# Three attentions: products with the values over pairs of query blocks

## Chip, core and metric

One core of one Trainium2 chip runs the whole program. The metric is device time in microseconds from the first to the last instruction, as the median of the runs.

## What is computed

Two transformer blocks, batch 1, 1024 tokens, width 1024, all in 32-bit floats. Three attentions stand in them, each worked in query blocks of 128 rows. The change touches only their last step, the product of the attention weights with the values:

```python
# first block, 16 heads of 64: stick-breaking attention, per query block i
a = where(mask, exp(log_beta + suffix), 0.0)        # mask: kpos < qpos
out = einsum('bhqk,bhkd->bhqd', a, vb)              # keys 0 .. end of block i
# second block: sliding window, 8 heads of 64, 2 groups of keys and values
probs = softmax(concat([scores, sink]))[..., :-1]   # keys of blocks n-1 and n
out = einsum('bnkgqs,bnskd->bnqkgd', probs, vb)
# second block: differential attention, 4 heads, values 128 wide
a = p[:, :, 0] - lam * p[:, :, 1]                   # two softmaxes, keys 0 .. end of block n
out = einsum('bhqs,bshe->bqhe', a, v)
```

Everything around them (projections, gates, a short convolution, a feed-forward part, norms) is the same before and after.

## The kernel before, in words

**Order of the work.** The program is written twice by `tile_body`: a dry pass learns how long each buffer lives, the second one writes the instructions. Both run a clock of their own (`Sched`, line 57 on): `note` (L153) adds an assumed cost to the engine of each instruction, and side tasks (generators) are woken when that clock says their inputs are there (`when`, L86; `turn` of `Sched`, L107). The main line of the program is the projections (`proj`, tile `pj`): between two of their matmuls, side tasks that are due slip in their own. So the costs in `note` fix the order of instructions on every engine, and on the chip each engine runs its list in that order, waiting where it must. Where the main line needs a side task to be done it stands still (`sch.until`): line 2272 for the first half of stick-breaking attention, 2281 for its second half, 2286 and 2292 for the two halves of the second block's attentions. While it stands, TensorE gets side work alone.

**The attentions.** `attention_1` runs `stick` (L1068) for tokens 0 to 511 and then 512 to 1023; `attention_2` runs `swa` (L1233) and `diff` (L1314) for the first half and then for the second. `crew` (L1035) keeps at most two to four units of work alive. A unit of `stick` is one of 8 pairs of heads `p`, a query block `i` and a head `h`. It makes scores on TensorE (tile `z`), two sigmoids on ScalarE (`om`, `be`; up to 512 keys both stand in one tile `ob`), a running product and a product on VectorE, turns the 128x128 blocks of `be` with TensorE (`turn`, L1009, tile `tr`), copies them to `aT` on ScalarE, and when both heads of a block are there multiplies:

```python
for kb in range(n):
    r = slice(0, 127 if kb == n - 1 else 128)
    for hh in range(2):
        mm(po[64 * hh:64 * hh + 64, (i % 4) * 128:(i % 4 + 1) * 128],
           lhsT=vt[r, kb * 128 + 64 * hh:kb * 128 + 64 * hh + 64],
           rhs=got[hh][r, kb * 128:(kb + 1) * 128], start=kb == 0, stop=kb == n - 1)
```

The values (`vt`, tile `vp`) are the stationary operand, 64 columns of the array for each head; `po` (tile `o`) holds four query blocks. `swa` does the same with two key blocks per query block and values from `vas`. `diff` uses all 128 columns: a unit is a head and a query block, with two softmaxes (scores and a row maximum in one VectorE instruction, shown as CUSTOM; `Exp` on ScalarE; scale-and-add on VectorE), then `turn` and the products. After a head's four blocks, `sub_norm` (L1399) sums squares with TensorE (tile `sm`), takes a root, spreads it (tile `rb`) and hands the head to the next projection. A plain 32-bit product is two TensorE instructions.

**Room.** Wide tiles come from 34 buffers; `room` (L312) holds a unit or a load back until enough are free.

Of the kernel before, what the change touches and what calls it, by code (L numbers as in the profile page):

```python
# [57 lines left out]
class Sched:  # L58
# [94 lines left out]
    def note(self, eng, op, out, args, extra=0.0):  # L153
# [111 lines left out]
def tile_body(  # L265
# [46 lines left out]
    def room(n, hold=0):  # L312

        while in_use[0] + n > N4:
            yield 0.4
        in_use[0] += hold
# [692 lines left out]
    def turn(src, n):  # L1009
# [10 lines left out]
        yield dst  # L1020
        return dst

    def fetched(loads, keys, need, fetch, tiles, ahead=1):
# [44 lines left out]
    def stick(live, half, width, rho):  # L1068
# [4 lines left out]
        def work(p, i, h):  # L1073
# [13 lines left out]
            for c0, c1 in CUTS[n]:  # L1087
# [17 lines left out]
            aT = yield from turn(be, n)  # L1105
            free()
            got = st.setdefault((p, i), {})
            got[h] = aT
            if len(got) < 2:
                return  # L1110
            if p not in st:
                yield from sch.a_bank()
# [10 lines left out]
            free(2 * (w > HT))  # L1123
            del st[p, i]
            st[p][1] += 1
            if st[p][1] == 3 and ("z", p, half) in flags:
# [106 lines left out]
    def swa(live, half, width, rho):  # L1233
# [15 lines left out]
        def work(t, n):  # L1249
# [35 lines left out]
            pT = yield from turn(p, 4)  # L1285
# [6 lines left out]
            blocks = [(0, n - 1), (1, n)] if n else [(0, 0)]  # L1292
            for a, (b, kb) in enumerate(blocks):
                for h in range(2):
                    mm(po[64 * h:64 * h + 64, (n % 4) * 128:(n % 4 + 1) * 128],
                       lhsT=vas[0][:, kb, 64 * g:64 * g + 64],
                       rhs=pT[:, (2 * h + b) * 128:(2 * h + b + 1) * 128],
                       start=a == 0, stop=a == len(blocks) - 1)
            st[t][1] += 1
            if st[t][1] == 4:  # L1300
                del loads[t], st[t]
                loads["done"].add(t)
# [11 lines left out]
    def diff(live, half, width, rho):  # L1314
# [43 lines left out]
        def work(h, i):  # L1358
            yield from arrived(loads, h)
            n = i + 1  # L1360
            w = n * 128
            yield from room(3 * (w > HT), 3 * (w > HT))
            p0, l0 = yield from softmax(h, i, 0)
            vec.tensor_scalar(out=p0[:, 0:w], in0=p0[:, 0:w], scalar1=l0[:, 0:1], scalar2=None, op0=ALU.mult)
            p1, l1 = yield from softmax(h, i, 1)
# [7 lines left out]
                loads["done"].add(h)  # L1373
                free(3 + half)
            yield p0
            aT = yield from turn(p0, n)
            free(w > HT)
            if h not in st:
                yield from sch.a_bank()
            if h not in st:  # L1380
# [7 lines left out]
            free(w > HT)  # L1388
            st[h][1] += 1
            if st[h][1] == 4:  # L1390
                del st[h], vts[h]
                free(half)
# [941 lines left out]
```

## Time and profile before

| what | value |
|---|---|
| median of 3 runs | 2580.68 us (2580.65 to 2581.55) |
| the profiled execution | 2582.41 us, its span 2580.6 us |
| granted TensorE clock, mean | 0.991 of full speed |
| TensorE matmuls busy | 97% of the span |
| VectorE, ScalarE, GpSimd busy | 69%, 49%, 19% |
| HBM traffic over the span | 253 GB/s |

A busy share is that of time in which at least one instruction of the engine was in flight. TensorE's matmuls overlap one another by their latency, so for the cost of one the distance between two starts counts, and not its length.

### The profile page before, as it was taken

What the parts mean: (1) busy time and instruction counts of PE and PEld (TensorE: products, weight loads), DVE (VectorE), ACT (ScalarE), POOL (GpSimd) and SP (SyncE); (2) the same over time, 40 slices, a digit from 0 to 9 for tenths busy, and PEclk for the clock granted to TensorE, in tenths of its full rate; (3) what the DMA queues carried; (4) which work ended last, traced back from release to release, by engine and by line L of the source; (5) the groups of instructions that cost most, each with busy time, mean ns of one, the idle gap of its engine ahead of it and who ended that gap; (6) DMA issues with size and microseconds to landing.
All of it is one profiled execution on the core that took longest, in us unless ns stands there. A gap on an engine that the chain in (4) does not pass through costs nothing.

```text
span 2580.6 us, 38805 instructions
## 1 busy us (share of the span) xinstructions
PE 2505.5 (97%) x13215; PEld 2057.5 (80%) x13215; DVE 1792.8 (69%) x3245; ACT 1255.7 (49%) x2529; POOL 490.0 (19%) x894
## 2 busy tenths in 40 slices
PE   7999999989999899998999999999999899999998
PEld 6888888879877677787888887888888678788887
DVE  7866666777697788986765556774666876677555
ACT  5311112555455677677664353564634634345442
POOL 0012112312101002331211321222222222221000
PEclk9999999999999999999999999999999999999999
DMA  9867869857897665775876978977886987978764
GB/s 283 264 190 201 203 214 280 235 185 249 279 274 222 204 163 157 221 192 140 250 217 160 262 209 261 260 226 220 200 237 217 237 225 235 238 225 252 226 201 130
DMA packets 541726, 570.43 MB, mean 221 GB/s; under 512 B 32910, under 2 KB 410008, under 8 KB 541528
## 3 DMA queue, kind: packets, MB, share of 16 engines
q1 hardware_dynamic: 482644, 381.99, 50.3%
q0 software_dynamic: 56528, 181.75, 25.3%
q10 hardware_dynamic: 2356, 4.21, 0.4%
q8 instruction: 104, 1.70, 0.3%
q14 instruction: 94, 0.77, 0.1%
HBM read 466.90 MB, written 186.91 MB: 253 GB/s over the span
## 4 chain that ended last, share of the span: by engine, by line
PE 65%; DVE 5%; DMA 3%; ACT 2%; issue 2%; SPq 0%; POOL 0%; DVEq 0%; ACTq 0%; POOLq 0%
PE pj L249 53%; PE o L249 4%; PE z L249 4%; PE tr L250 3%; DVE om L250 2%; PE pv L249 1%; DMA wr<-sg_d2g 1%; DVE be L250 1%; DVE wl L250 1%; DMA wr<-in_b_w_out_dram 1%; DVE ob L250 1%; DVE act L250 0%; DVE fa L250 0%; ACT om L250 0%; ACT be L250 0%
## 5 line engine op out<-in xcount | busy, mean ns | idle before, releaser
L249 PE MATMUL pj<-act,wh 128*128 128x512 f32 (+1 forms) x5680 | 1783.0, 395 | 26.2 <-DVE act L250 16.8
L249 PEld LDWEIGHTS pj<-act,wh 128*128 128x128 f32 x5680 | 1046.2, 189 | 256.8 <-DVE act L250 22.9
L249 PE MATMUL pj<-act,wl 128*128 128x512 f32 (+1 forms) x2840 | 1113.7, 392 | 0.0
L249 PEld LDWEIGHTS pj<-act,wl 128*128 128x128 f32 x2840 | 536.2, 189 | 123.1 <-DVE wl L250 1.3
L250 DVE TENSOR_TENSOR wl<-wr,wh 128x512 fp32r<-128x512 f32 x714 | 476.4, 679 | 169.7 <-ACT wh L250 156.2
L250 ACT CAST wh<-wr 128x512 fp32r<-128x512 f32 x714 | 425.8, 617 | 177.6 <-PE pj L249 41.8
L250 POOL COPY paced<-wl 128x1 f32<-128x1 f32 x256 | 114.7, 448 | 881.6 <-DVE wl L250 840.9
L250 ACT COPY aT<-tr 128x512 f32<-128x512 f32 (+3 forms) x272 | 128.7, 501 | 162.0 <-PE tr L250 159.6
L249 PE MATMUL z<-kd,qs 128*128 128x512 f32 (+2 forms) x704 | 166.4, 350 | 1.7 <-DVE o L250 0.7
L250 DVE SCALAR_TENSOR_TENSOR acc<-mw,silu_c,acc 128x512 f32<-128x512 f32 x196 | 146.5, 748 | 2.7 <-DMA mw<-in_a_mod_w_dram 0.3
L249 PEld LDWEIGHTS z<-kd,qs 128*128 128x128 f32 x704 | 113.7, 190 | 19.4 <-issue 7.2
L250 DVE TENSOR_TENSOR_SCAN om<-om,begin 128x640 f32<-128x640 f32 (+3 forms) x64 | 120.6, 1885 | 10.2 <-ACT om L250 10.2
L249 PEld LDWEIGHTS o<-aT,vp 128*64 128x64 f32 (+2 forms) x1440 | 99.9, 149 | 22.8 <-issue 14.5
L249 PE MATMUL o<-aT,vp 128*64 128x128 f32 (+2 forms) x1440 | 116.3, 280 | 0.4 <-ACT aT L250 0.4
L250 ACT COPY u<-pj 128x512 f32<-128x512 f32 x46 | 27.0, 588 | 157.8 <-PE pj L249 80.1
L250 ACT ACTIVATE p<-p,t 128x256 f32<-128x256 f32 (+7 forms) x128 | 81.3, 636 | 20.7 <-DVE t L250 20.5
L250 ACT ACTIVATE sq<-xn 128x512 f32<-128x512 f32 x48 | 30.6, 637 | 110.6 <-DVE xn L250 110.5
L250 ACT ACTIVATE om<-z 128x384 f32<-128x384 f32 (+2 forms) x128 | 69.3, 542 | 22.6 <-PE z L249 19.0
L249 PE MATMUL pj<-wh,act 128*128 128x256 f32 x448 | 79.9, 281 | 0.0
L250 PE MATMUL tr<-ident,be 128*128 128x128 f32 x416 | 61.1, 283 | 18.1 <-DVE be L250 17.7
L250 PEld LDWEIGHTS tr<-ident,be 128*128 128x128 f32 x416 | 47.3, 143 | 32.4 <-DVE be L250 20.7
L250 DVE TENSOR_TENSOR be<-be,om 128x639 f32<-128x639 f32 (+3 forms) x64 | 66.2, 1034 | 6.7 <-ACT sq L250 0.5
(252 smaller groups left out, 2757.5 us busy)
## 6 DMA issues: line engine op xcount, KB each, us to landing
wr<-in_w_in_dram SPq DMA_DIRECT2D x136, 256.0 KB
mw<-in_w_ada_dram SPq DMA_DIRECT2D x96, 256.0 KB
wr<-in_a_w_in_dram SPq DMA_DIRECT2D x80, 256.0 KB
al<-dn_d SPq DMA_DIRECT2D x77, 256.0 KB
wr<-in_w_up_dram SPq DMA_DIRECT2D x66, 256.0 KB
sw_d<-in_w_down_dram POOLq DMA_DIRECT2D x48, 352.0 KB, 5.0
wr<-in_b_w_qz_dram SPq DMA_DIRECT2D x64, 256.0 KB
qs<-q_d SPq DMA_DIRECT2D x64, 256.0 KB
```

What stands on the lines that cost most here:

```text
L249: return f(out, *value, **kw)
L250: return f(out=out, **kw)
```

## The change

A pair of query blocks, `i0` and `i0 + 1`, shares one product per key block: the stationary values are loaded once and 256 columns (both query blocks) stream past. The last key block is seen by the second query block alone and keeps 128 columns. `aT` is laid out with the two query blocks side by side (`turn_pair`, `pair_block`), the products start when both blocks (in `stick` of both heads) are turned, and the tiles of a pair are held that long (`pair_tiles`, `room`). In `stick` the last column of `be` is set to zero by a ScalarE instruction, so that all 128 rows can be used. `swa` runs three products per pair and head in place of four. The costs that `note` assumes for 32-bit products are new too. The diff, cut:

```diff
-                d = n / 600 if args[0].free_size() == 128 else n / 1070
+                d = max(n / 1100, 0.213) if args[0].free_size() == 128 else max(n / 2200, 0.108)
...
+    def pair_tiles(i):
+        return (i % 8) // 2 if i < 4 else 2
+    def pair_new(i):
+        return [sml(name="aT")] if i == 0 else [big([2 * HT], name="aT", held=True) for _ in range(pair_tiles(i))]
+    def pair_block(tiles, kb, j):
+        return tiles[kb // 4][:, kb % 4 * 256 + 128 * j:kb % 4 * 256 + 256]
+    def turn_pair(src, n, tiles, j):
...
+            dst = tiles[b0 // 4].rearrange("p (k j q) -> p k j q", j=2, q=128)
+            sca.copy(out=dst[:, 0:b1 - b0, j, :], in_=ps[:, 0:(b1 - b0) * 128].rearrange("p (k q) -> p k q", q=128))
...
-            yield from room(1 if w <= HT else 3, int(w > HT))
+            i0, j = i & ~1, i % 2
+            extra = 0 if j else pair_tiles(i)
+            while j and (p, i0, h) not in st:
+                yield 0.4
+            yield from room((1 if w <= HT else 2) + extra, extra)
...
+            act(out=be[:, w - 1:w], in_=be[:, w - 1:w], func=ACTF.Copy, scale=0.0)
...
-            for kb in range(n):
-                r = slice(0, 127 if kb == n - 1 else 128)
+            for kb in range(i0 + 2):
+                j0 = int(kb > i0)
                 for hh in range(2):
-                    mm(po[64 * hh:64 * hh + 64, (i % 4) * 128:(i % 4 + 1) * 128],
-                       lhsT=vt[r, kb * 128 + 64 * hh:kb * 128 + 64 * hh + 64],
-                       rhs=got[hh][r, kb * 128:(kb + 1) * 128], start=kb == 0, stop=kb == n - 1)
+                    mm(po[64 * hh:64 * hh + 64, (i0 % 4 + j0) * 128:(i0 % 4 + 2) * 128],
+                       lhsT=vt[:, kb * 128 + 64 * hh:kb * 128 + 64 * hh + 64],
+                       rhs=pair_block(got[hh], kb, j0), start=kb == 0, stop=kb > i0)
...
+            runs = [(n0, 1, 0, 2), (n0 - 1, 0, 0, 1), (n0 + 1, 3, 1, 1)] if n0 else [(0, 0, 0, 1), (0, 2, 1, 1), (1, 3, 1, 1)]
+            for a, (kb, c, q0, nq) in enumerate(runs):
                 for h in range(2):
...
+                    mm(po[64 * h:64 * h + 64, (n0 % 4 + q0) * 128:(n0 % 4 + q0 + nq) * 128],
+                       lhsT=vas[0][:, kb, 64 * g:64 * g + 64], rhs=pT[:, h, c * 128:(c + nq) * 128],
+                       start=a == 0 or (n0 == 0 and a == 1), stop=a == 2 or n0 + a == 0)
...
-            yield from room(3 * (w > HT), 3 * (w > HT))
+            i0, j = i & ~1, i % 2
+            extra = 2 * (w > HT) + (0 if j else pair_tiles(i))
+            while j and (h, i0) not in st:
+                yield 0.4
+            yield from room(extra, extra)
...
-            for kb in range(n):
-                mm(po[:, (i % 4) * 128:(i % 4 + 1) * 128], lhsT=vt[:, kb * 128:(kb + 1) * 128],
-                   rhs=aT[:, kb * 128:(kb + 1) * 128], start=kb == 0, stop=kb == n - 1)
+            for kb in range(i0 + 2):
+                j0 = int(kb > i0)
+                mm(po[:, (i0 % 4 + j0) * 128:(i0 % 4 + 2) * 128], lhsT=vt[:, kb * 128:(kb + 1) * 128],
+                   rhs=pair_block(aT, kb, j0), start=kb == 0, stop=kb > i0)
```

**Place 1, TensorE, stick-breaking, the last pair of heads of the first half, query blocks 0 and 1.** Before, the products of block 0 stand alone and those of block 1 (four like them) follow later:

```order
L249 MATMUL o_8609<-aT_8540,vp_8310 64x128
L249 MATMUL o_8609<-aT_8595,vp_8310 64x128
L250 MATMUL tr_8616<-ident,ob_8564 128x128 x2
L249 MATMUL z_8621<-kd_8308,qs_8312 128x384 x2
L249 MATMUL pj_8626<-act_5892,wh_8459 128x512 x2
L249 MATMUL pj_8626<-act_5892,wl_8535 128x512
L250 MATMUL tr_8637<-ident,ob_8582 128x128 x2
```

Now the four products of both blocks stand together, behind the scores (`z`) of block 2:

```order
L249 MATMUL z_8684<-kd_8351,qs_8355 128x384 x2
L249 MATMUL z_8691<-kd_8351,qs_8356 128x384 x2
L249 MATMUL o_8697<-aT_8618,vp_8353 64x256
L249 MATMUL o_8697<-aT_8664,vp_8353 64x256
L249 MATMUL o_8697<-aT_8618,vp_8353 64x128
L249 MATMUL o_8697<-aT_8664,vp_8353 64x128
L249 MATMUL z_8705<-kd_8351,qs_8355 128x512 x2
L250 MATMUL tr_8716<-ident,ob_8683 128x128 x3
```

What moved: two groups of `o` became one, with as many columns in all, and the projections between them are gone here: from `tr_8665`, three rows ahead of the piece, 77 matmuls follow one another without a `pj`, into the second half's first units; before, the longest such run here had 56.

**Place 2, TensorE, the end of the differential attention's second half** (`p` are weights before they are turned). Before, the last products, the squares (`sm`) and what stands between them:

```order
L249 MATMUL o_19090<-aT_19263,vp_18726 128x128 x8
L249 MATMUL pj_19293<-act_18015,wh_19185 128x512 x2
L249 MATMUL pj_19293<-act_18015,wl_19210 128x512
L249 MATMUL pj_19293<-act_18031,wh_19185 128x512 x2
L249 MATMUL pj_19293<-act_18031,wl_19210 128x512
L249 MATMUL pj_19328<-act_17971,wh_19208 128x512 x2
L249 MATMUL pj_19328<-act_17971,wl_19252 128x512
L249 MATMUL pj_19328<-act_17973,wh_19208 128x512 x2
L249 MATMUL pj_19328<-act_17973,wl_19252 128x512
L250 MATMUL sm_19344<-ident,sq_19316 128x128 x4
L249 MATMUL pj_19328<-act_18015,wh_19208 128x512 x2
L249 MATMUL pj_19328<-act_18015,wl_19252 128x512
```

Now the same end; the first `pj` is that of the projection behind line 2292:

```order
L250 MATMUL tr_19072<-ident,p_18987 128x128 x4
L249 MATMUL z_19078<-kd_18241,qs_18245 128x512 x2
L250 MATMUL tr_19082<-ident,p_18987 128x128 x3
L250 MATMUL tr_19094<-ident,p_19046 128x128 x4
L250 MATMUL tr_19100<-ident,p_19046 128x128 x4
L249 MATMUL o_19035<-aT_19070,vp_18238 128x256 x4
L249 MATMUL o_19035<-aT_19071,vp_18238 128x256 x3
L249 MATMUL o_19035<-aT_19071,vp_18238 128x128
L250 MATMUL sm_19121<-ident,sq_19118 128x128 x4
L250 MATMUL rb_19140<-ident,t_19138 128x128 x4
L249 MATMUL pj_19155<-act_15646,wh_18788 128x512 x2
```

What moved: in the old order the projections of `up_first` (L1588) lie between the steps of this chain; in the new one they have all been issued earlier, and from the second-softmax scores of head 3's block 4 up to `rb` only one group of three `pj` is left.

## Rows read from the trace of the kernel before

**Rows 1.** The page's busy times: us, share of the span, instructions.
```profile
PE 2505.5 (97%) x13215; PEld 2057.5 (80%) x13215; DVE 1792.8 (69%) x3245; ACT 1255.7 (49%) x2529; POOL 490.0 (19%) x894
```

**Rows 2.** Stretches; columns: us, busy us (count) of PE, PEld, DVE, ACT, POOL, PEclk, DMA.
```profile
640.00:880.00 240.00, 237.10 (x1429) 188.43 (x1427) 177.87 (x294) 124.82 (x289) 28.20 (x50) 1.00 0.85 255
880.00:1180.00 300.00, 279.35 (x2036) 231.26 (x2036) 262.41 (x296) 219.38 (x480) 60.73 (x84) 0.98 0.63 177
1700.00:1860.00 160.00, 160.00 (x831) 135.53 (x830) 97.16 (x223) 92.95 (x163) 37.95 (x76) 1.00 0.71 200
```

**Rows 3.** Timeline of PE; columns: start us, length us, engine, line, operation, names, form, count.
```profile
992.76 0.48 PE L249 MATMUL row<-row,ones 1*128 1x264 f32 x1
993.09 0.38 PE L249 MATMUL row<-row,ones 1*128 1x264 f32 x1
...
1150.36 0.28 PE L249 MATMUL pv<-wh,act 128*128 128x256 f32 x1
1150.48 0.28 PE L249 MATMUL pv<-wl,act 128*128 128x256 f32 x1
```

**Rows 4.** Chain of waits by time, end of one differential head: start us, us, what.
```profile
1767.34 0.44 PE sm L250 x4
1767.78 3.44 PE pj L249 x15
1771.21 0.44 PE rb L250 x4
```

**Rows 5.** Groups by form, PE; after the bar: busy us, mean ns of one, idle before.
```profile
L249 PE MATMUL o<-aT,vp 128*128 128x128 f32 x288 | 37.0, 275 | 0.0
L249 PE MATMUL pj<-wh,act 128*128 128x256 f32 x448 | 79.9, 281 | 0.0
L250 PE MATMUL vt<-ident,rows 95*128 95x95 f32 x1 | 0.2, 245 | 0.0
L250 PE MATMUL vt<-ident,rows 66*128 66x66 f32 x1 | 0.2, 221 | 0.0
```

**Rows 6.** Timeline of PE around two groups of stick-breaking products.
```profile
972.80 1.53 PE L249 MATMUL o<-aT,vp 128*64 128x128 f32 x24
974.26 0.73 PE L249 MATMUL z<-kd,qs 128*128 128x512 f32 x2
...
1142.61 0.62 PE L249 MATMUL pj<-act,wh 128*128 128x512 f32 x2
1143.07 0.40 PE L249 MATMUL pj<-act,wl 128*128 128x512 f32 x1
1143.39 1.75 PE L249 MATMUL o<-aT,vp 128*64 128x128 f32 x28
1145.08 0.33 PE L250 MATMUL tr<-ident,be 128*128 128x128 f32 x1
```

**Rows 7.** Groups by form, DVE and ACT, 1190 to 1860 us.
```profile
L250 DVE CUSTOM_DVE_ANT_0 p<-z,DD,t 128x512 f32<-128x512 f32 x8 | 6.0, 751 | 1.2
L250 DVE CUSTOM_DVE_ANT_0 p<-z,DD,t 128x256 f32<-128x256 f32 x8 | 3.9, 483 | 0.9
L250 DVE SCALAR_TENSOR_TENSOR p<-p,t,p 128x1024 f32<-128x1024 f32 x4 | 5.1, 1286 | 0.1
L250 DVE SCALAR_TENSOR_TENSOR p<-p,t,p 128x640 f32<-128x640 f32 x4 | 3.5, 885 | 0.1
L250 DVE TENSOR_SCALAR p<-p,t 128x1024 f32<-128x1024 f32 x4 | 3.0, 754 | 0.1
L250 DVE RECIPROCAL t<-t 128x1 f32<-128x1 f32 x64 | 10.0, 157 | 3.2 <-ACT p L250 3.1
L250 DVE TENSOR_REDUCE t<-sm 128x4 f32<-128x512 f32 x11 | 7.6, 691 | 18.9 <-PE sm L250 18.9
L250 ACT ACTIVATE p<-p,t 128x1024 f32<-128x1024 f32 x8 | 9.2, 1155 | 4.4 <-DVE t L250 4.3
L250 ACT COPY aT<-tr 128x512 f32<-128x512 f32 x61 | 35.6, 591 | 65.0 <-PE tr L250 64.9
```

More of the change, by code (lines that the diff above doesn't have):

```diff
@@ L1021, in turn @@
         return dst
+    def pair_tiles(i):
[5 more added lines that the diff above has]
+    def turn_pair(src, n, tiles, j):
+        for b0 in range(0, n, 4):
+            b1 = min(n, b0 + 4)
+            yield from sch.a_bank()
+            ps = bank("tr")
+            for b in range(b0, b1):
+                ten.transpose(out=ps[:, (b - b0) * 128:(b - b0 + 1) * 128],
+                              in_=src[:, b * 128:(b + 1) * 128], identity=ident)
+            dst = tiles[b0 // 4].rearrange("p (k j q) -> p k j q", j=2, q=128)
+            sca.copy(out=dst[:, 0:b1 - b0, j, :], in_=ps[:, 0:(b1 - b0) * 128].rearrange("p (k q) -> p k q", q=128))
+        yield tiles
     def fetched(loads, keys, need, fetch, tiles, ahead=1):
@@ L1080, in work @@
             qb = q[:, :, (i % 4) * 128:(i % 4 + 1) * 128]
-            yield from room(1 if w <= HT else 3, int(w > HT))
+            i0, j = i & ~1, i % 2
[3 more added lines that the diff above has]
+            yield from room((1 if w <= HT else 2) + extra, extra)
+            if not j:
+                st[p, i0, h] = []
             if w <= HT:
@@ L1104, in work @@
             yield be
-            aT = yield from turn(be, n)
+            aT = st[p, i0, h]
+            if not aT:
+                aT.extend(pair_new(i0))
+            yield from turn_pair(be, n, aT, j)
             free()
-            got = st.setdefault((p, i), {})
-            got[h] = aT
-            if len(got) < 2:
+            done = st.setdefault((p, i0), [])
+            done.append((h, j))
+            if len(done) < 4:
                 return
@@ L1116, in work @@
             yield vt
-            for kb in range(n):
-                r = slice(0, 127 if kb == n - 1 else 128)
+            got = [st.pop((p, i0, hh)) for hh in range(2)]
+            for kb in range(i0 + 2):
+                j0 = int(kb > i0)
                 for hh in range(2):
-                    mm(po[64 * hh:64 * hh + 64, (i % 4) * 128:(i % 4 + 1) * 128],
-                       lhsT=vt[r, kb * 128 + 64 * hh:kb * 128 + 64 * hh + 64],
-                       rhs=got[hh][r, kb * 128:(kb + 1) * 128], start=kb == 0, stop=kb == n - 1)
[L1123 to L1126, printed above, removed]
+                    mm(po[64 * hh:64 * hh + 64, (i0 % 4 + j0) * 128:(i0 % 4 + 2) * 128],
+                       lhsT=vt[:, kb * 128 + 64 * hh:kb * 128 + 64 * hh + 64],
+                       rhs=pair_block(got[hh], kb, j0), start=kb == 0, stop=kb > i0)
+            free(2 * pair_tiles(i0))
+            del st[p, i0]
+            st[p][1] += 2
+            if st[p][1] == 2 and ("z", p, half) in flags:
                 zs[p, half] = sml(name="zl")
@@ L1284, in work @@
             yield p
-            pT = yield from turn(p, 4)
+            n0, j = n & ~1, n % 2
+            if (t, n0) not in st:
+                yield from room(1)
+            if (t, n0) not in st:
+                st[t, n0] = [big([2, HT], name="aT"), []]
+            pT, done = st[t, n0]
+            yield from sch.a_bank()
+            ps = bank("tr")
+            for b in range(4):
+                ten.transpose(out=ps[:, b * 128:(b + 1) * 128], in_=p[:, b * 128:(b + 1) * 128], identity=ident)
+            sca.copy(out=pT[:, :, 256 * j:256 * j + 256], in_=ps.rearrange("p (h c) -> p h c", h=2))
+            yield pT
+            done.append(j)
+            if len(done) < 2:
+                return
             if t not in st:
@@ L1291, in work @@
             g = t // 2
-            blocks = [(0, n - 1), (1, n)] if n else [(0, 0)]
-            for a, (b, kb) in enumerate(blocks):
+            runs = [(n0, 1, 0, 2), (n0 - 1, 0, 0, 1), (n0 + 1, 3, 1, 1)] if n0 else [(0, 0, 0, 1), (0, 2, 1, 1), (1, 3, 1, 1)]
+            for a, (kb, c, q0, nq) in enumerate(runs):
                 for h in range(2):
[L1295 to L1299, printed above, removed]
+                    mm(po[64 * h:64 * h + 64, (n0 % 4 + q0) * 128:(n0 % 4 + q0 + nq) * 128],
+                       lhsT=vas[0][:, kb, 64 * g:64 * g + 64], rhs=pT[:, h, c * 128:(c + nq) * 128],
+                       start=a == 0 or (n0 == 0 and a == 1), stop=a == 2 or n0 + a == 0)
+            del st[t, n0]
+            free()
+            st[t][1] += 2
             if st[t][1] == 4:
@@ L1361, in work @@
             w = n * 128
-            yield from room(3 * (w > HT), 3 * (w > HT))
+            i0, j = i & ~1, i % 2
[3 more added lines that the diff above has]
+            yield from room(extra, extra)
+            if not j:
+                st[h, i0] = []
             p0, l0 = yield from softmax(h, i, 0)
@@ L1375, in work @@
             yield p0
-            aT = yield from turn(p0, n)
+            aT = st[h, i0]
+            if not aT:
+                aT.extend(pair_new(i0))
+            yield from turn_pair(p0, n, aT, j)
             free(w > HT)
+            done = st.setdefault((h, i0, "n"), [])
+            done.append(j)
+            if len(done) < 2:
+                return
             if h not in st:
@@ L1384, in work @@
             yield vt
-            for kb in range(n):
-                mm(po[:, (i % 4) * 128:(i % 4 + 1) * 128], lhsT=vt[:, kb * 128:(kb + 1) * 128],
-                   rhs=aT[:, kb * 128:(kb + 1) * 128], start=kb == 0, stop=kb == n - 1)
-            free(w > HT)
-            st[h][1] += 1
+            del st[h, i0], st[h, i0, "n"]
+            for kb in range(i0 + 2):
+                j0 = int(kb > i0)
+                mm(po[:, (i0 % 4 + j0) * 128:(i0 % 4 + 2) * 128], lhsT=vt[:, kb * 128:(kb + 1) * 128],
+                   rhs=pair_block(aT, kb, j0), start=kb == 0, stop=kb > i0)
+            free(pair_tiles(i0))
+            st[h][1] += 2
             if st[h][1] == 4:
```

## Prediction

> **What bounds the kernel now.** The page first: TensorE has a matmul in flight for 97% of the span, VectorE is busy for 69% and ScalarE for 49% [rows 1]. So TensorE's own work sets the time, and what others cost shows as its idle time. Next the stretches in which the attentions run: idle is 240 - 237.1 = 2.9 us in the first half of stick-breaking, 300 - 279.35 = 20.7 us in its second half, and nothing at the end of the differential attention [rows 2]. In the second of them VectorE is busy for 262 of 300 us: there TensorE arrives at the turning of `be` before VectorE has it. Last the single instruction, since the change rests on what a product of 128 or 256 columns costs.
>
> **Does a longer product save time? The diff's new costs say so: a full-width product of 256 columns at 0.233 us, one of 128 at 0.213.** That holds if the load of the stationary values is what a product waits for. The trace has no plain 32-bit product of 256 columns, but one of 264, in two instructions: the second starts at 993.09, the first at 992.76 [rows 3]. In these 0.33 us lie the first one's load (0.11, the distance at which short 32-bit instructions follow each other: 0.44 us for 4 in [rows 4]) and its stream: 0.22 us for 264 columns, 0.83 ns for each. The lengths tell the same. A 32-bit transpose of 66 columns takes 221 ns, one of 95 takes 245: 24 ns for 29 columns, again 0.83 [rows 5]. Carried on, 128 columns would take 272 ns and 264 columns 385; the products of 128 take 275 [rows 5] and the second instruction of the 264 takes 0.38 us [rows 3]. The projections' reduced format streams 256 columns in about the same 281 ns [rows 5]: a plain 32-bit column costs two of theirs. So at 128 columns load and stream are both 0.11 us and hide each other, and a pair's 256 columns will stream for 0.21 us per instruction, twice what one block took. The columns are as many as before. The products themselves save next to nothing: 0.6 us, with 0 and 1.3 as bounds (an instruction of 128 columns takes 0.11 us where 0.83 x 128 = 106 ns are stream, and there are some 250 fewer such steps).
>
> **What the change does save.** Stick-breaking and window products use 64 columns of the array at a time. A group of 24 such instructions (12 pairs side by side) takes 974.26 - 972.80 = 1.46 us until the next matmul starts, one of 28 takes 1145.08 - 1143.39 = 1.69 [rows 6]. That is 0.11 us a pair of instructions and some 0.15 us for the group. Before the group, the last `pj` takes 0.32 us until the first product starts, where `pj` instructions follow each other at 0.23 [rows 6]. So each change between the two shapes costs some 0.09 + 0.15 = 0.25 us, whatever is in the group. The order has 93 such groups before and 48 now: 45 x 0.25 = **-11.2 us**, all on TensorE.
>
> **What it moves, first place: stick-breaking.** The order keeps the same scores and turns but puts more projections between them: from the last product of the first half to the last group of the second half, 693 matmuls of 512 columns in place of 489, and 192 `pv` in place of 165. That is 204 x 0.23 + 27 x 0.12 = 50 us more TensorE work under the same VectorE work [rows 3, 6]. Each product, too, takes longer on the chip than the new costs assume, so VectorE and ScalarE get ahead of the order. VectorE's share in the stretch falls from 87% to about 80% (262 us plus some 20 for the added projections, over 350). At 74% (the first half: 177.87 of 240) TensorE idled for 1.2% of the time, at 87% for 6.9% [rows 2]. Between them, 3% of 350 us is 10.5 us: **-10 us** from 20.7. Bounds: 0, if the waits only change place, and -16.5, if the stretch becomes as calm as the first half. The 128 new ScalarE instructions that clear one column lie beside VectorE's running product; I cost them at nothing. If that cover is gone, each holds up what is behind it on ScalarE by at most an `aT` copy's 0.59 us [rows 7], and a turn waits that much more.
>
> **Second place: the end of the first half.** With 77 matmuls in a row and no `pj` (56 before), two more query blocks of the last pair of heads have nothing beside them. **+2 us** (0 to 6): their VectorE work is close to TensorE's own there.
>
> **Third place, and the largest: the end of the differential attention.** Here the main line stands still (line 2292) and only head 3 is left. From the second scores of its block 4 to `rb`, TensorE's order holds 87 matmuls: 28 score matmuls at 0.12 to 0.23, 42 turns and sums at 0.11, 14 products, most at 0.43 (two instructions of 0.21), three `pj` at 0.23. That is 16 us in all. The chain beside it is longer. VectorE has, in order: 14 reductions of scores (0.48 to 0.75, with a read-out of 0.08 each: 10.0 us), four scale-and-adds (0.885 to 1.286: 4.3), three scalings (0.754 the longest: 2.1), 11 small ones with 0.157 (1.7), and 3.8 for head 2's norm and the last gate of `up_first`: 22 us [rows 7]. It waits some 3.5 us for ScalarE's exponentials (1.155 the longest) and for scores. After the last scale-and-add come turns and two copies (1.8), the products behind them (2.7), copy and square of `o` (1.4), `sm`, reduction (0.69), root, `rb` (3.1): 9 us. Together 34.5 us against 16 us of own work: 18 us idle. In the old order the same chain is covered, 3.44 us of projections between `sm` and `rb` alone [rows 4], and the stretch has no idle time [rows 2]. Gaps bring the clock down as well: the stretch with 20.7 us idle was granted 0.98 on average, the others 1.00 [rows 2], which means about 12 us of it at 1.2 GHz. If the same happens here, turns and products of the chain take up to twice their time: 2 us (0 to 5). So **+20 us**, bounds 12 (VectorE's instructions overlapping, waits half as long) and 25.
>
> **The sum**, against the profiled execution's 2582.4: -11.2 - 0.6 - 10 + 2 + 20 = +0.2, so 2582.6. The median of the runs is 1.7 us lower than that execution: **2581 us**, no change within what can be measured (0.2%, 5.2 us).
>
> **The rivals.**
> *The products do get shorter.* If a 32-bit instruction streamed one column per cycle and waited for its load, one of 256 columns would cost the 0.12 us that lie between two `pv` instructions of 256 [rows 3]. Stick-breaking and window: before 348 pairs of products, two instructions each, at 0.11, 76.6 us; now 140 at 0.12 and 68 at 0.11, 48.6 us. Differential: 288 x 0.11 = 31.7 before, 128 x 0.12 + 32 x 0.11 = 18.9 now. That is -41 us, part of it lost in waits: about 2545. Against it stand the 264 columns. The Trainium skill has this as a rule ("TensorE: Matmul & The Clock Gate", Back-to-back issue gap): N / 2.4 + 2.5 ns warm, no type named, 109 ns at 256. The same skill says on the other side that true 32-bit products take four passes ("FP8 and Floating Point Precision", TensorE Precision Notes), 427 ns for a product of 256 as an estimate; the 0.22 us per instruction agree with the second. Chance 5%.
> *Slower: the chain at the end costs its upper bound and stick-breaking keeps its waits.* For: one in-order list without filler cannot hide a late step. Against: the 50 us of added cover. 2580.7 - 11.2 - 0.6 + 25 + 4 = 2598, the case reaching from 2586. It decides once the idle time at the end passes the 22 us that groups and stick-breaking save together. Chance 29%.
> *Faster: stick-breaking becomes calm (-16.5) and the end costs 13 us.* 2580.7 - 11.8 - 16.5 + 2 + 13 = 2567, the case reaching to 2575.5. For: VectorE has fewer rows per us of TensorE's time. Against: the waits of the second half are chains of score, sigmoid, running product and turn, which more cover shortens only where it stands in the right place. Chance 28%.
> That the products are not paired is excluded by the order: 344 products of 256 columns stand in it, 280 of 64 array columns and 64 of 128.
>
> **How the numbers follow.** The forecast (2575.5 to 2586) has 38%. Faster: 28 + 5 = 33%; slower: 29%. The ends of all bounds are 2564 and 2600; the range that leaves out 2 in 10 is 2567 to 2595, since the case near 2545 takes part of what is left out below.
>
> **What would show it.** Products of 256 columns with a length of about 380 ns and starts 0.21 to 0.22 apart confirm the stream, 281 and 0.12 the first rival. TensorE's idle time between 880 us and the last stick-breaking product should fall to about 10 us, and 15 to 20 us should appear between the last `pj` of `up_first` and `rb` of head 3, with VectorE and ScalarE as releasers. If that stretch shows under 10 us, or if idle time appears where I named none (window attention, loads of the next head), the forecast was right by luck or wrong.

## The result, and the profile after

The changed kernel takes 2623.98 us (median of 4 runs, 2622.74 to 2632.09), the kernel before 2581.11 beside it (2580.65 to 2586.86): ratio 1.0168, 95% interval 1.0142 to 1.0193. That is 43 us slower; the forecast was 2581 us, its range went up to 2595. The profiled execution took 2624.67 us, its span 2622.9.

First the page's busy times of the changed kernel; the line answers to [rows 1].

```profile
PE 2510.7 (96%) x12527; PEld 2046.4 (78%) x12527; DVE 1793.8 (68%) x3244; ACT 1281.6 (49%) x2660; POOL 491.1 (19%) x893
```

TensorE is busy 5 us longer with 688 instructions fewer, and its idle time grew from 75 to 112 us. Where, the stretches tell. They are cut at TensorE's own instructions, the same ones in both kernels: first half of stick-breaking; second half; window and differential attention, first half; projections until the next attention; the second half of those attentions, to head 3's `rb`; the rest. Columns as in [rows 2]: stretch, us, busy us (count) of PE, PEld, DVE, ACT, POOL, granted clock, DMA share, GB/s. The kernel before, in stretches not shown so far:

```profile
680.40:875.70 195.30, 192.52 (x1154) 148.74 (x1152) 155.87 (x257) 112.26 (x267) 21.64 (x40) 1.00 0.87 257
875.70:1208.70 333.00, 306.22 (x2258) 254.81 (x2254) 276.98 (x330) 241.19 (x526) 67.59 (x94) 0.97 0.64 175
1208.70:1335.60 126.90, 126.64 (x750) 105.03 (x747) 92.81 (x312) 86.39 (x222) 23.18 (x51) 1.00 0.74 217
1335.60:1504.20 168.60, 166.66 (x828) 138.94 (x826) 86.02 (x160) 72.39 (x132) 40.55 (x70) 0.99 0.80 219
1504.20:1865.30 361.10, 361.10 (x1898) 298.92 (x1898) 232.32 (x570) 192.57 (x386) 85.46 (x172) 1.00 0.81 229
1865.30:2572.30 707.00, 693.32 (x3128) 564.17 (x3126) 466.16 (x803) 308.65 (x573) 128.44 (x241) 0.99 0.77 222
```

The changed kernel, the same stretches:

```profile
680.80:882.00 201.20, 193.04 (x1034) 147.59 (x1034) 156.94 (x259) 123.70 (x333) 21.61 (x40) 0.99 0.90 265
882.00:1276.30 394.30, 363.44 (x2166) 292.51 (x2164) 308.73 (x415) 280.38 (x660) 80.61 (x117) 0.96 0.60 168
1276.30:1393.70 117.40, 110.31 (x572) 89.43 (x569) 79.87 (x254) 74.76 (x179) 16.97 (x38) 0.97 0.71 209
1393.70:1521.30 127.60, 127.34 (x669) 107.57 (x667) 67.64 (x136) 57.19 (x105) 32.72 (x57) 1.00 0.85 223
1521.30:1899.90 378.60, 363.07 (x1756) 297.77 (x1755) 232.53 (x567) 195.11 (x387) 84.16 (x173) 0.98 0.80 223
1899.90:2613.90 714.00, 694.46 (x3124) 564.69 (x3124) 465.49 (x800) 308.70 (x572) 132.25 (x242) 0.99 0.76 217
```

Idle time rose from 2.8 to 8.2, 26.8 to 30.9, 0.3 to 7.1, 1.9 to 0.3, 0 to 15.5 and 13.7 to 19.5 us. It grew in five of the six stretches; the prediction named two of them, the end of stick-breaking's first half and that of the differential attention, and let it fall in a third, the second half of stick-breaking. The lengths themselves don't compare, since projections moved between stretches. For that the table below sets against each stretch its *own work*: TensorE's instructions in it, each counted at the distance between two starts of its form at the granted clock of 1.00 (512 columns 0.232 us, 384 0.175, 256 in the reduced formats 0.119, a 32-bit transpose or an instruction of a product 0.109 for 128 columns and 0.216 for 256, half of these for two products side by side; with the 0.211 found below no entry moves by more than 1 us). What is over holds idle time, shape changes and time at the lower clock; us:

| over own work | stick 1st | stick 2nd | diff 1st | between | diff 2nd | rest |
|---|---|---|---|---|---|---|
| before | 16.0 | 51.6 | 4.2 | 4.2 | 5.5 | 20.9 |
| changed | 19.8 | 56.2 | 13.7 | 0.6 | 25.9 | 28.6 |
| changed, KEEP 5 (e9) | 21.9 | 34.8 | 9.8 | 0.5 | 10.0 | 22.3 |
| before, KEEP 8 (e13) | 15.6 | 54.5 | 5.6 | 4.9 | 42.7 | 19.0 |

**A product of 256 columns.** The groups by form, in answer to [rows 5]:

```profile
L249 PE MATMUL o<-aT,vp 128*64 128x256 f32 x512 | 63.9, 390 | 0.1
L249 PE MATMUL o<-aT,vp 128*128 128x256 f32 x128 | 34.8, 420 | 0.4 <-ACT aT L250 0.4
L249 PE MATMUL o<-aT,vp 128*64 128x128 f32 x128 | 13.1, 277 | 0.0
```

And TensorE's timeline of the changed kernel around one group of stick-breaking products and one of differential products (start, length), in answer to [rows 6]; both groups end with a key block of 128 columns, which the merged row doesn't say:

```profile
928.91 0.40 PE L249 MATMUL pj<-act,wl 128*128 128x512 f32 x1
929.23 3.46 PE L249 MATMUL o<-aT,vp 128*64 128x256 f32 x32
932.62 2.14 PE L249 MATMUL z<-kd,qs 128*128 128x384 f32 x12
...
1737.19 3.40 PE L249 MATMUL o<-aT,vp 128*128 128x256 f32 x16
1740.36 0.70 PE L249 MATMUL pj<-act,wh 128*128 128x512 f32 x2
```

The second group lasts 3.17 us: less 0.22 for its two instructions of 128 columns, 14 take 2.95, 0.211 each, the stream of the prediction. The first lasts 3.39: 14 pairs side by side at 0.211 and two at 0.11 make 3.17, and some 0.2 us are the shape change, after the same 0.32 us at its entry as before.

**The end of the differential attention.** TensorE's waits from 1852 to 1903 us of the changed kernel (who waited for whom: total, times, longest); before, the stretch up to `rb` had no idle time at all (its line above), and [rows 4] shows 15 `pj` between `sm` and `rb` at the end of an earlier head:

```profile
PE tr L250 <- DVE p L250: 9.8, 3, 3.9
PE tr L250 <- DVE t L250: 2.3, 1, 2.3
PE rb L250 <- DVE t L250: 2.2, 1, 2.2
PE sm L250 <- ACT sq L250: 1.2, 1, 1.2
```

The turns wait four times for VectorE (for the weights, or for the small values `t` behind them), up to 3.9 us each, and the sum and the spreading behind the last products wait too. The stretches around it:

```profile
1855.00:1862.00 7.00, 7.00 (x38) 6.25 (x37) 3.82 (x13) 3.51 (x7) 0.97 (x2) 1.00 1.01 279
1862.00:1890.00 28.00, 15.88 (x71) 12.79 (x69) 19.36 (x54) 17.72 (x30) 6.13 (x13) 0.78 0.61 130
1890.00:1901.00 11.00, 7.59 (x29) 5.96 (x28) 1.69 (x7) 3.73 (x7) 0.00 (x0) 0.80 0.09 25
```

All 15.5 us of idle time lie here. The granted clock is 1.00 in the first of these stretches, where TensorE has no gap, and 0.78 and 0.80 in the other two, so some 17 of the 39 us after 1862 ran at the lower level of 1.2 GHz (28 x 2 x 0.22 + 11 x 2 x 0.20). Why so late? SyncE's timeline of the keys' loads for the four heads (issue time, length) tells. The kernel before:

```profile
1611.58 1.24 SPq L250 DMA_DIRECT2D kd<-kd_d  x2
1653.11 4.62 SPq L250 DMA_DIRECT2D kd<-kd_d  x2
1663.63 5.01 SPq L250 DMA_DIRECT2D kd<-kd_d  x2
1776.68 1.28 SPq L250 DMA_DIRECT2D kd<-kd_d  x2
```

The changed kernel:

```profile
1623.09 1.12 SPq L250 DMA_DIRECT2D kd<-kd_d  x2
1670.56 2.27 SPq L250 DMA_DIRECT2D kd<-kd_d  x2
1771.57 2.70 SPq L250 DMA_DIRECT2D kd<-kd_d  x2
1777.57 5.01 SPq L250 DMA_DIRECT2D kd<-kd_d  x2
```

Before, only head 3's load comes late; now head 2's does too. Two heads come in after 1771 us where one came. These loads stand in `fetched` (L1047), which asks `room` for the load's five wide buffers and KEEP = 7 more. `room` holds back while the program is written: until there is a place for the load, the head's units can't be placed either, and projections take the places between. With two heads left for the end, the projections run out before the heads do, as the new order of place 2 shows. The prediction's sum has no term for it; its last sentence names "loads of the next head" only as a place where idle time would count against it.

### The profile page after: what moved, and what is told of

The parts are those of the page before. It is cut to its first block, busy times and chain, and to the rows that moved or that the text cites. A ratio compares the mean times of both kernels' runs of the same rounds, so it can differ in the third digit from the quotient of the medians.

```text
span 2622.9 us, 37438 instructions
## 1 busy us (share of the span) xinstructions
PE 2510.7 (96%) x12527; PEld 2046.4 (78%) x12527; DVE 1793.8 (68%) x3244; ACT 1281.6 (49%) x2660; POOL 491.1 (19%) x893
## 4 chain that ended last, share of the span: by engine, by line
PE 49%; DVE 6%; ACT 2%; DMA 2%; issue 1%; POOL 0%; SPq 0%; DVEq 0%; ACTq 0%; POOLq 0%
PE pj L249 39%; PE o L249 3%; PE z L249 2%; PE tr L250 2%; PE pv L249 1%; DVE fa L250 1%; DVE om L250 1%; DMA wr<-sg_d0g 1%; DMA dn_d<-fa 1%; DVE p L250 1%; DVE wl L250 1%; DVE be L250 1%; DMA wr<-sg_d2g 0%; DVE act L250 0%; ACT om L250 0%
## 5 line engine op out<-in xcount | busy, mean ns | idle before, releaser
L250 POOL COPY paced<-wl 128x1 f32<-128x1 f32 x256 | 121.0, 473 | 901.7 <-DVE wl L250 817.0
L249 PE MATMUL z<-kd,qs 128*128 128x384 f32 (+2 forms) x704 | 166.8, 353 | 0.8 <-issue 0.8
L249 PE MATMUL o<-aT,vp 128*64 128x256 f32 (+3 forms) x800 | 109.9, 373 | 0.5 <-ACT aT L250 0.4
L249 PEld LDWEIGHTS o<-aT,vp 128*64 128x64 f32 (+1 forms) x800 | 77.4, 153 | 36.3 <-issue 6.8
L250 DVE TENSOR_REDUCE t<-sm 128x4 f32<-128x512 f32 x40 | 27.6, 689 | 67.9 <-PE sm L250 67.9
```

What stands on the lines that cost most here:

```text
L249: return f(out, *value, **kw)
L250: return f(out=out, **kw)
```

## The experiments

Theory A at the start: the pairs make units late, and TensorE waits where a stage ends without projections. Theory B: the new assumed costs spoil the order.

**e1 and e2, the costs alone and the pairs without them** (`note`; e1 puts the new line into the kernel before, e2 the old one into the changed kernel).

```diff
-                d = max(n / 1100, 0.213) if args[0].free_size() == 128 else max(n / 2200, 0.108)
+                d = n / 600 if args[0].free_size() == 128 else n / 1070
```

> The kernel before with the new line of assumed costs alone; nothing is paired. Theory A (the pairing itself makes units late and buffers held; the waits stand where a stage ends and no projections are left) expects no change: 2581 us, within 2576 to 2587. Theory B (the new costs, which take a paired product for half of what it lasts, spoil the order of all the attentions) expects a large part of the 43 us lost: 2600 us or more. In TensorE's order the end of the first half of stick-breaking has 10.7 us of work without a projection in place of 7.7, the end of the differential attention 5.1 us as in the kernel before.

> The changed kernel with the old line of assumed costs, which for 256 columns gives 0.43 and 0.24 us, what the trace measured. Theory A expects 2615 to 2630 us, since the pairs are as late as in the changed kernel and TensorE's order still has 13.3 us without a projection at the end of the differential attention (14.4 in the changed kernel). Theory B expects 2570 to 2590 us: pairs fewer shape changes and no spoilt order.

Measured: e1 0.9991 (0.9982 to 1.0001), e2 2626.67 us, 1.0169 (1.0154 to 1.0184). Theory B falls.

**e3 and e8, more projections for the ends.**

```diff
-M_BR = 5
-M_WO = 6
+M_BR = 7
+M_WO = 8
```

e8, in the changed kernel too: `N_Z = 4`, `N_G = 5`, `M_BR = 9`, `M_WO = 10`, and three of `run_g1`'s jobs ahead of the wait for the first half of the second block's attentions.

> The changed kernel with two more blocks of up-projections kept for the time of the second half's attentions (M_BR 7 in place of 5, M_WO 8 in place of 6). TensorE's order then has 5.0 us without a projection at the end of the differential attention in place of 14.4. Theory A expects the 20 us of that place back: 2604 us (2600 to 2609), the stretch from the first window unit of the second half to the last head's rb with 5 to 8 us over its own work in place of 25.9. The rival, that VectorE's chain is late wherever it stands and the wait only moves, expects 2615 us or more. The other losses (12 us in the stick-breaking stages, 10 at the end of the first half of differential attention) should stay.

> The changed kernel with projections kept for all ends: two more of z ahead of the end of stick-breaking's first half (N_Z 4), two more gates ahead of the end of its second half (N_G 5), three gates moved ahead of the end of the first half of differential attention, and M_BR 9. If the losses sit where projections ran out: 14 us at the last end and 10 us at the first half of differential attention go, some 5 at the first half of stick-breaking, so 2624 - 29 = 2595 us (2588 to 2603). If they only move, as half of them did with two more blocks of up-projections (2616.5 us), 2610 us or more. What VectorE's queue costs inside stick-breaking, about 15 us, should stay.

Measured: e3 2616.52 us, 1.0126 (1.0108 to 1.0143); e8 2621.27, 1.0145 (1.0130 to 1.0160). Both miss: the place is right and the cure wrong. The last two stretches of e8:

```profile
1525.00:1921.40 396.40, 396.07 (x1929) 325.57 (x1929) 247.38 (x593) 220.02 (x423) 94.84 (x190) 1.00 0.83 230
1921.40:2611.00 689.60, 656.40 (x2935) 528.86 (x2934) 448.82 (x771) 291.62 (x541) 117.45 (x221) 0.98 0.74 214
```

The end of the differential attention has almost no idle time left (0.3 us, 15.5 in the changed kernel), and the rest has 33.2 us in place of 19.5: the projections moved forward were missing behind it, where TensorE waits from 2020 to 2100 us for the inputs of the next ones, 26 us where the changed kernel waits 8:

```profile
PE pj L249 <- ACT act L250: 18.7, 7, 7.9
PE pj L249 <- DVE act L250: 7.5, 8, 1.6
```

**e4, e6, e7, one attention at a time** (the other two as before, old costs).

> Pairs in stick-breaking attention alone, window and differential attention as before, old costs. Shape changes fall from 93 groups to 61: 32 x 0.25 = 8 us less. Theory A expects the changed kernel's losses of the stick-breaking stages (5.7 and 4.6 us over before, the shape changes already counted in) and none of the later ones: 2591 us, within 2585 to 2597. If the prediction's step on stick-breaking held (calmer, because more projections lie between), it would be 2581 - 8 - 10 = 2563 us. If pairs in stick-breaking also starve the later stages of projections, 2600 us or more; TensorE's order, with 5.1 us without a projection at the end, speaks against it.

> Pairs in window attention alone, old costs. 13 groups fewer of the other array shape: 13 x 0.25 = 3.3 us less, 2577.5 us, within 2574 to 2581, if its pairs (one wide buffer each) wait for nothing new; TensorE's order has no stretch without projections that the kernel before hasn't. If the 10 us lost at the end of the first half of differential attention come from the window units, 2585 us or more.

> Pairs in differential attention alone, old costs; it changes no array shape and saves no columns, so nothing is to be gained. TensorE's order has no long stretch without projections at the end of its second half. Theory A: its losses are those of the two ends alone, which depend on how many projections earlier stages used up, so here 2580 to 2588 us. The rival, that its pairs are late by themselves: half of the 24 us that the changed kernel lost beyond pairs in stick-breaking alone, 2592 us or more.

Measured: e4 2600.28 us, 1.0067 (1.0052 to 1.0082), above its range; e6 1.0002 (0.9992 to 1.0011); e7 1.0015 (1.0006 to 1.0025). Alone, window and differential pairs cost next to nothing, and the three make 17 + 0 + 4 of the 43 us. The rest comes only when they are together. e6 shows none of the 3.3 us that its shape changes were expected to be worth. In e7 head 2's load comes at 1707.13 us, 44 us later than before and 64 earlier than in the changed kernel. e4 loses its time in the second half of stick-breaking:

```profile
877.00:1309.70 432.70, 395.58 (x2327) 316.87 (x2325) 316.61 (x431) 297.58 (x685) 79.14 (x131) 0.96 0.61 174
```

Its own work there is 368 us, 86 more than in the kernel before, and 65 us are over it, 13 more.

**e5, e11, e12, what it is in stick-breaking.** e5 reserves buffers as the pairs do and pairs nothing; e11 issues both blocks' products together and pairs nothing; e12 pairs and leaves out the cleared column.

```diff
 # e5
-            yield from room(1 if w <= HT else 3, int(w > HT))
+            yield from room((1 if w <= HT else 2) + extra, extra)
...
 # e11
-            if len(got) < 2:
+            if len(got) < 4:
                 return
...
 # e12
-            act(out=be[:, w - 1:w], in_=be[:, w - 1:w], func=ACTF.Copy, scale=0.0)
```

> The kernel before, with nothing paired, but its stick-breaking units reserve wide buffers as the pairs do: those of both query blocks before the first one starts, given back when the second one's products are done. Theory A, in its form after the four runs before (what the pairs cost in stick-breaking is the buffers they hold: units start in bunches, VectorE idles first and is late afterwards): at least half of what pairs in stick-breaking alone cost, 18 us and the 8 us of shape changes that they save, so 2595 to 2610 us. The rival (the products' waiting for four units is what costs): 2579 to 2587 us, as before.

> The kernel before, but in stick-breaking the products of two query blocks and both heads are issued together, still 128 columns each, from separate tiles, without the cleared column. This has the pairs' delay and their 32 shape changes fewer, and neither the 256 columns nor the extra ScalarE instruction. If the delay of the products and the order that follows from it cost the 17 us (and the 8 us that the shape changes give), 2594 to 2605 us, like pairs in stick-breaking alone (2600). If the column cleared on ScalarE costs them, 2582 - 8 = 2574 us, within 2568 to 2580.

> Pairs in stick-breaking alone, without the instruction that clears the last column of be (so each query also sees its own position). The 128 instructions take 0.204 us each, 26 us of ScalarE, between the sigmoids of one unit and those of the next. If they hold up the chain, 2574 to 2588 us; if they lie beside other work, as the prediction had it, 2596 to 2603 us as with them (2600).

Measured: e5 1.0007 (0.9997 to 1.0016); e11 2599.21 us, 1.0064 (1.0049 to 1.0079); e12 2601.06, 1.0071 (1.0054 to 1.0088). The reservation in stick-breaking costs nothing, and that form of theory A falls. The cleared column costs nothing either (e4 with it 2600.28), though it takes 26 us of ScalarE. What costs is that the products are issued together: e11, without a single product of 256 columns, is as slow as the pairs. The load of the last keys tells the two apart as well: in e5 it is issued 34 us after the one ahead of it (1079.66 and 1114.16), in e11 87 us (1089.79 and 1176.68), in the kernel before 36.

**e9, e10, e13, the loads.** Theory C, from the loads above: pairs push the next head's load back behind `room`.

```diff
-KEEP = 7
+KEEP = 5
```

e9 is the changed kernel with 5, e10 the kernel before with 5, e13 the kernel before with 8.

> The changed kernel with KEEP 5 in place of 7: the loads of the next head's keys, queries and values may start when two wide buffers fewer are free. Theory C: at the end of the differential attention the pairs' buffers make the load of head 2 wait until the old load of head 3 would come, so two heads instead of one are left for the end, and the projections run out first. Then this one number brings the last end back: no long stretch without projections there, 20 us less and nothing taken from a later stage: 2604 us (2599 to 2610), the stage of the second half's attentions with under 10 us over its own work in place of 25.9. Rival: VectorE's chain at the end is late whatever the loads do, or the wait moves on, as with more up-projections: 2612 us or more.

> The kernel before with KEEP 5, to tell what this number does without pairs. Its last head too waits for its load, but behind it projections are left. All theories: within 5 us of the kernel before, 2577 to 2588 us.

> The converse: the kernel before, nothing paired, with KEEP 8, so that its own loads wait for one wide buffer more. TensorE's order then has 29.0 us without a projection at the end of the differential attention (14.4 in the changed kernel, where they cost 20 us), since three heads are left behind late loads. Theory C: a loss without any pair, at that end: 2605 to 2630 us, with the loads of the last heads in the trace 40 us or more after those of the kernel before. Rival (the pairs themselves lengthen the end): 2577 to 2590 us.

Measured: e9 2582.90 us, 0.9997 (0.9987 to 1.0006); e10 2578.82, 0.9986 (0.9977 to 0.9995); e13 2622.33, 1.0154 (1.0139 to 1.0169). One number takes back all 43 us, twice what was expected, and one buffer more makes nearly as large a loss in a kernel without a pair. Against the kernel before with 5 (e10), the pairs with 5 cost 4 us. The second halves of stick-breaking and of the other attentions in e9:

```profile
886.70:1289.60 402.90, 385.42 (x2323) 311.13 (x2323) 319.61 (x451) 300.22 (x702) 92.54 (x127) 0.98 0.68 187
1500.70:1791.60 290.90, 286.30 (x1446) 236.54 (x1446) 205.62 (x522) 158.51 (x332) 61.22 (x124) 0.99 0.79 225
```

The loads of heads 2 and 3 in e9:

```profile
1669.66 1.03 SPq L250 DMA_DIRECT2D kd<-kd_d  x2
1687.59 1.58 SPq L250 DMA_DIRECT2D kd<-kd_d  x2
```

and those of the four heads in e13, the last 58 us after that of the kernel before:

```profile
1663.75 1.34 SPq L250 DMA_DIRECT2D kd<-kd_d  x2
1749.06 1.35 SPq L250 DMA_DIRECT2D kd<-kd_d  x2
1755.69 4.06 SPq L250 DMA_DIRECT2D kd<-kd_d  x2
1834.53 1.84 SPq L250 DMA_DIRECT2D kd<-kd_d  x2
```

with the stretch of e13 that ends at head 3's `rb`, 26.7 us idle where the kernel before has none:

```profile
1506.90:1907.50 400.60, 373.90 (x1905) 307.89 (x1904) 233.56 (x572) 201.02 (x392) 92.50 (x185) 0.97 0.78 221
```

In stick-breaking the last pair of heads shows it too. The last two loads of its keys, second half, in the changed kernel and then in e9; the kernel before has 36 us between the two (1071.51 and 1107.69):

```profile
1106.29 0.82 SPq L250 DMA_DIRECT2D kd<-k_d  x2
1176.31 1.47 SPq L250 DMA_DIRECT2D kd<-k_d  x2
```

```profile
1098.20 1.26 SPq L250 DMA_DIRECT2D kd<-k_d  x2
1141.34 1.09 SPq L250 DMA_DIRECT2D kd<-k_d  x2
```

**e14 to e18, what pairs are worth with the loads in time.** All have KEEP 5: pairs in stick-breaking (e14), there and in the window (e15), in the window (e16), and e15 and e16 with the new costs (e17, e18).

> Pairs in stick-breaking alone, with KEEP 5. With KEEP 7 they cost 17 us, and issuing the products together without pairs cost the same. Theory C also for this place (units wait for the keys of the next pair of heads, then come in bunches): 2572 to 2585 us, the 8 us of shape changes showing in part. If the late products spoil the order of VectorE's work by themselves, 2592 us or more.

> Pairs in stick-breaking and window attention, differential attention as before, old costs, KEEP 5: all 45 shape changes fewer and no pairs where they save none. Theory C: not above stick-breaking alone with KEEP 5, 2570 to 2582 us.

> Pairs in window attention alone with KEEP 5: the kernel before with KEEP 5 was 2579 us; 13 shape changes fewer are 3.3 us, of which none was seen at KEEP 7: 2574 to 2580 us. If it is under the kernel before with KEEP 5, this is the version that beats both kernels.

> Pairs in stick-breaking and window attention, KEEP 5, with the new line of assumed costs; against the same kernel with the old line (2595 us) only that line differs. The changed kernel with KEEP 5 (all pairs, new line) had 35 us over its own work in the second half of stick-breaking, the kernel with the old line 65. If the new line, which takes a paired product for half of what it lasts, lets VectorE and ScalarE run ahead of the order there, as the prediction's step on stick-breaking said, this one has 35 to 45 us there too and 2567 to 2582 us. If the pairs in differential attention made that difference, 2590 to 2600 us.

> Pairs in window attention alone, KEEP 5, with the new line of costs: without pairs in stick-breaking the new line alone moved nothing (0.9991 with KEEP 7), so 2567 to 2576 us as with the old line (2571).

| run | median us | ratio, 95% interval |
|---|---|---|
| e14 | 2591.93 | 1.0035 (1.0022 to 1.0048) |
| e15 | 2594.73 | 1.0043 (1.0026 to 1.0060) |
| e16 | 2571.08 | 0.9958 (0.9943 to 0.9973) |
| e17 | 2579.81 | 0.9988 (0.9978 to 0.9997) |
| e18 | 2580.94 | 0.9990 (0.9980 to 0.9999) |

e14 and e15 miss: with the loads in time, stick-breaking's pairs still cost 9 us and more under the old costs (13 and more against e10). e16 is better than expected, e18 worse. Between e15 and e17 only the line of costs differs. The second half of stick-breaking in e15:

```profile
880.10:1275.30 395.20, 356.38 (x2128) 284.70 (x2128) 303.80 (x407) 282.93 (x655) 76.50 (x118) 0.96 0.61 169
```

and in e17:

```profile
883.50:1288.00 404.50, 385.93 (x2325) 311.80 (x2323) 319.46 (x451) 300.09 (x702) 93.11 (x127) 0.98 0.67 187
```

38.8 us idle against 18.6, and 65.5 over own work against 36.3, with the last keys issued at the same time (1139.95 and 1139.21 us). So the stretch needs both: over own work it has some 62 to 65 us with the old costs, whether the last keys come late (e2, e4) or not (e14, e15), 56 with the new costs and late keys (the changed kernel), and 35 to 36 with the new costs and keys in time (e9, e17). The new line, which moved the total neither in the kernel before (e1) nor with late loads (e2), helps these pairs once the loads are in time. e16 beats both kernels, by 0.42% against the kernel before. KEEP alone makes some 3.6 us of that (e10), and 3.3 would be expected of its 13 shape changes. But most of its gain lies in the second half of stick-breaking, where nothing but its first window products is paired, 41 us over own work in place of 51.6:

```profile
875.60:1200.70 325.10, 305.62 (x2272) 254.24 (x2270) 278.42 (x339) 242.15 (x538) 67.26 (x93) 0.98 0.66 181
```

e18, the same but for the costs, is 10 us slower and has 51 there. So part of e16's gain hangs on the order as a whole, and no run separates it.

## Why the prediction was wrong, point by point

**The products save next to nothing: right.** 0.211 us for an instruction of 256 columns, 0.21 forecast. With it falls the rival of 2545 us. The Trainium skill ("TensorE: Matmul & The Clock Gate", Back-to-back issue gap) gives a rule that makes 109 ns at 256 columns, without naming a type. For 32-bit products this trace differs from it, and for the reduced format the 0.12 us of [rows 3] are near it.

**45 shape changes at 0.25 us: right in count and size**, by the groups' own starts. But e6 shows that 13 fewer can vanish in a new order.

**Stick-breaking -10 us: wrong.** This is the step that failed: "The order keeps the same scores and turns but puts more projections between them", and from that VectorE's share of the stretch gives TensorE's idle time. The projections were there, 338 us of own work in place of 281, and VectorE's share fell as forecast, from 83% (276.98 of 333.00) to 78% (308.73 of 394.30). Yet idle time rose from 26.8 to 30.9 us, and 56.2 us stand over own work, where -10 and some 4 for 16 shape changes would have left 38. The share doesn't set the waits: at 77 to 79% they are 17.5 us (e9, 402.90 - 385.42), 30.9 and 38.8 (e15). Nor does the amount of projections: e4 and e9 have the same 368 us of own work, and 65 and 34.8 over it. What is left is where projections and turns stand in the order, which the loads and the costs both set. With the loads in time and the new costs the step's result comes out, 34.8 (e9) and 36.3 (e17). So its other reason, costs assumed too low, has a part in it (e15 against e17); alone, with late loads, it doesn't do it. The size had a slip too: read straight between the two rows it took, 80% gives 4% of 350 us and -7 in place of -10.

**The end of the first half, +2 (0 to 6): too small.** Over own work it is +3.8, although some 16 shape changes (4 us) went from this stretch; about +8 without them. Late loads are not its cause (21.9 with KEEP 5). With the old costs the same pairs have 16.3 (e2), but e12, with the old costs too, has 19.3: the cause stays open.

**The end of the differential attention +20: right in size** (25.9 - 5.5 = 20.4, of which 15.5 idle; 18 idle and 2 of clock forecast), and wrong in what it hangs on. It was read as the price of the pairs' order, where it was that of one load issued 108 us later than before (1771.57 against 1663.63, head 2). With the load at 1669.66 us (e9) 4.5 us of it are left, and without any pair but with late loads (e13) it is 37.

**Not named: +9.5 at the end of the first half of differential attention and +7.7 behind the attentions.** By the prediction's own last sentence, idle time where none was named makes it wrong. In e9 both are smaller, +5.6 and +1.4; in e17, with KEEP 5 as well, the second is about +8, so late loads are not shown to be its cause.

**What was left out.** The change's `room` was quoted, and counted only as what a unit waits for. Nobody asked who else queues at the same counter: in the second halves `fetched` asks for 9 to 12 buffers, a unit for one to four, so what is held longer should be paid by the loads first. The Trainium skill ("Perfetto Trace Analysis", Identifying Performance Opportunities) says that a gap which repeats for a stretch can mean too few buffers for the next tile. At the end of the differential attention the runs agree with the cause (e9, e13) and not with the form: the buffer that is short shows first as a late load (1771.57 us), some 90 us ahead of the idle time. The rival on the slower side (2598 us) had the right sign, but only in the places that the prediction knew. The ScalarE instruction that clears a column, costed at nothing, cost nothing (e12).

**What stays open.** KEEP also stands in front of the outputs of two norms (L408), and no run moves the one without the other; that the loads moved is seen in the trace. Which tiles fill the room when head 2's load waits was not traced: that it is the pairs' is argued from their lines with `room`, and in stick-breaking e5 speaks against it, where the same reservation delayed no load. Nor is it shown why issuing the products together costs stick-breaking 17 us under the old costs (e11). That the order of VectorE's work is the reason is not shown. All pairs with the old costs and KEEP 5 were not run.

## What to carry to other kernels

Where a change holds buffers longer, list everyone who waits at the same counter, the prefetches first since they ask for most, and look in the trace of before for a load that already comes late: here head 3's, 113 us after head 2's, and one buffer less for the loads cost 39 us without any pair (e13). Projections that hide waits are a fixed stock, and moving them to one end bares another (e8). Try the one number that governs the prefetch before judging the idea: with 7 the pairs cost 43 us, with 5 they cost 4 (2582.90 against 2578.82 us). None of the 11 us that fewer shape changes promised shows in the total even then.

## Not expected of the hardware

Waits were paid for twice. At the end of the differential attention 15.5 us of idle time went with a granted clock of 0.78 and 0.80 over 39 us, and a group of 16 instructions of products, which lasts 3.40 us at 1737 us, lasted 5.63 us at 1890:

```profile
1890.17 5.63 PE L249 MATMUL o<-aT,vp 128*128 128x256 f32 x16
```

The forecast had 2 us for the clock there; what the stretch gained over own work beyond its idle time is about 5 (20.4 - 15.5), an estimate, since shape changes are in it too.
